# Three MLP down projections as seven block products a quarter (Strassen), with weight sums made on the chip

## The chip, the cores and the metric

One core of one Trainium2 chip runs the whole kernel in one launch. Times are device microseconds. The kernel before has a median of 2088.71 us over three runs (2087.34 to 2089.89). All sizes are float32; "fp32r" is the form in which TensorE takes a float32 operand in a single pass.

## The reference

Two layers of a first block and one layer of a second one work on x of 512 tokens by 1024 channels. Each layer ends in an MLP with 4096 hidden channels, and only the three MLPs are changed:

```python
# layers 0 and 1
h = rms_norm(x, norm_pre_mlp[i])
y = jnp.square(jax.nn.relu(h @ w_up[i])) @ w_down[i]
x = x + rms_norm(y, norm_post_mlp[i])
# layer 2 (the second block), then a last norm
hm = rms_norm_2(x, g_mlp[l])
x = x + jnp.square(jax.nn.relu(hm @ w_up[l])) @ w_down[l]
```

## The kernel before

A product of float32 accuracy is made from three passes (`mm3`): every operand is split into hi (its rounding, written by ScalarE) and lo (the exact rest, written by VectorE, `split` at L241 and L242), and hi·hi, hi·lo and lo·hi are added up in a bank of PSUM. A pass is a matmul of 128 x 128 by 128 x 512.

`mlp` takes the 4096 hidden channels in four quarters f of 1024. A quarter has an up phase of eight blocks of 128 channels (`project`; 8 x 24 = 192 matmuls), each followed by ScalarE's relu (L514), VectorE's square (L515) and a split into the `big` tiles, which hold the down product's stationary side. Then comes the down phase: four token tiles by two halves of 512 output columns, each over eight K-blocks in three passes, 8 x 24 = 192 matmuls into the banks named `acc`. In quarters 0 to 2 `out_gemm` runs one column half after the other; in quarter 3 `last_down` runs both halves of a token tile in turn, so that tile 0 is finished first. Weights come in chunks of 512 KB through three landing tiles ws and are split into WB = 4 pairs of tiles wh, wl. The queue of SyncE (SP) issues all loads.

In layers 0 and 1 the sums over quarters are kept in four tiles y (ScalarE's copy at f = 0, VectorE's `y += acc`, L536, after that). In quarter 3 each finished half is squared and summed (L319), multiplied by the gain (L542), and with both halves done `add_normed` takes GpSimd's power (L326) and adds y / rms to x (L469). `after` then runs the next mixer's norm of that token tile (L343), its transposes on TensorE (L267) and their split into h. `issue_late` sets where in TensorE's order a tile's transposes stand: those of tile t-1 behind the last product of tile t. In layer 2 the sums go straight into x (L527). Engines work their instructions in the order given, so a waiting instruction holds back everything behind it on its engine.

Of the kernel before, what the change touches and what calls it, by code (L numbers as in the profile page):

```python
# [20 lines left out]
NT = T // P  # L21
# [8 lines left out]
# ---------------------------------------------------------------- host layout  # L30
def ws(w):
    """[K, N] -> [N/128][128 of K][K/128 * 128 of N]: a block of columns as the stationary side."""
    k, n = w.shape
    return np.ascontiguousarray(
        w.reshape(k // P, P, n // P, P).transpose(2, 1, 0, 3)
    ).reshape(n // P, P, -1)


def xs(w, kt, n):
    """[K, N] -> [N/n][K/(128 kt)][128][kt * n]: a block of columns as the moving side."""  # L40
    k, nn = w.shape
    return np.ascontiguousarray(
        w.reshape(k // (kt * P), kt, P, nn // n, n).transpose(3, 0, 2, 1, 4)
    ).reshape(nn // n, k // (kt * P), P, kt * n)

# [30 lines left out]
def arrange(a):  # L76
# [22 lines left out]
    for i in range(2):  # L99
# [4 lines left out]
        o[f"wd{i}"] = xs(f["w_down"][i], 2, 512)  # L104
# [16 lines left out]
    o["wd2"] = xs(f["w_down_2"][0], 2, 512)  # L121
# [48 lines left out]
# ---------------------------------------------------------------- device  # L170
class Net:
# [21 lines left out]
    def load_x(self, src, gain=True, tiles=range(NT)):  # L193
        """x, and room for the gain of the next mixer's norm"""
# [13 lines left out]
    # -- small helpers  # L208
# [30 lines left out]
    def split(self, hi, lo, src, engine=None):  # L239
        """src = hi + lo: hi is src rounded to what one pass carries, lo the exact rest."""  # L240
# [19 lines left out]
    def mm(self, out, lhs, rhs, start, stop, more=False):  # L260
        """more: the bank's sums are added to again once they have been read"""
# [29 lines left out]
    def sooner(self, n):  # L291
        """the instructions within go before the n before them where both can"""
# [7 lines left out]
    def mm3(self, out, lhs, rhs, start, stop):  # L300
        """lhs, rhs: (hi, lo); out += lhs^T rhs to float32's accuracy."""
# [5 lines left out]
    # -- norms; np is the pool of their scratch  # L307
# [13 lines left out]
    def rstd(self, np_, ss):  # L321
        """ss: [128, 2], the halves' sums of squares / 1024 -> 1 / sqrt(mean + eps)"""
# [9 lines left out]
    def norming(self, np_, src, g, hi, lo, t, bank="tp", keep=True, junk=None):  # L332
        """src: the two halves of 128 rows; their normalised transpose goes to columns t of hi, lo."""
# [19 lines left out]
    def issue_late(self, t, last):  # L353
        """the transposes of token tile t go behind `last` in TensorE's order"""
# [14 lines left out]
    def prenorm(self, np_, gname, tiles, bank="tp", kept=False):  # L369
        """the normalised rows of x, transposed and split, tile by tile through the function it returns"""  # L370
# [8 lines left out]
    # -- matrix products  # L379
# [73 lines left out]
    def big_chunks(self, tp):  # L453
        """room for chunks of weights, two in a pair of big tiles"""
# [8 lines left out]
    # -- the end of a layer  # L463
    def add_normed(self, np_, t, yg, ss):
        """x += yg / rms, yg the products with the gain"""
        r = self.rstd(np_, ss)
        for j in range(2):
            x = self.xhalves(t)[j]
            self.nc.vector.scalar_tensor_tensor(out=x, in0=yg[:, j * 512:(j + 1) * 512], scalar=r, in1=x,  # L469
                                                op0=ALU.mult, op1=ALU.add)  # L470

    def mix_out(self, tp, wname, mixed, gname, corder, after, lead=3, store=True):
        """x += [norm of] mixed^T W_out"""
# [4 lines left out]
        for nh in range(2):  # L478
            def done(t, p):
# [3 lines left out]
                else:  # L483
                    if nh == 0:
                        y[t] = tp.tile([P, D], F32, name="y", tag="y", bufs=4)
# [16 lines left out]

    def mlp(self, tp, i, h, post, after):
# [3 lines left out]
        y, ss = {}, {}  # L507
        for f in range(4):
            u = [[tp.tile([P, 4, T], F32R, name="big", tag="big", bufs=8) for _ in range(2)] for _ in range(2)]

            def relu2(b, p):
                b -= f * 8
                r = tp.tile([P, T], F32, name="relu", tag="relu", bufs=2)
                nc.scalar.activation(r, p, AF.Relu)  # L514
                nc.vector.scalar_tensor_tensor(out=r, in0=p, scalar=0.0, in1=r, op0=ALU.max, op1=ALU.mult)  # L515
                self.split(u[b // 4][0][:, b % 4, :], u[b // 4][1][:, b % 4, :], r)
            self.project(f"wu{i}", range(f * 8, f * 8 + 8), h, relu2, 0 if f else 5)

            def lhs(k, t):
                c = slice(t * P, (t + 1) * P)  # L520
                return u[k // 4][0][:, k % 4, c], u[k // 4][1][:, k % 4, c]
            dones = []
            for nh in range(2):
                def done(t, p, f=f, nh=nh):
                    c = slice(nh * 512, (nh + 1) * 512)
                    if g is None:
# [1033 lines left out]
```

## Time and profile before

| | |
|---|---|
| runs shown | 2087.34, 2088.71, 2089.89 us |
| profiled execution: span | 2085.1 us |
| TensorE (PE) busy | 2050.3 us, 98% |
| VectorE (DVE) busy | 1184.1 us, 57% |
| ScalarE (ACT) busy | 949.4 us, 46% |
| GpSimd (POOL) busy | 111.8 us, 5% |
| bytes moved by DMA | 200.07 MB, mean 96 GB/s |

The span is that of one execution under the profiler; the runs shown are whole executions, and the median is 3.6 us above that span. "PE" rows are matmuls, "PEld" the loads of their stationary side, which overlap them. A matmul's own duration is its latency: the next one starts before it ends. In a timeline row with a count the second number is the time from the first start to the last end. DRAM traffic is far from filling the queues (one hardware queue carries 198.29 MB and is busy for 29.7% of the span).

### The profile page before, as it was taken

The numbers are of one execution on the slowest core, as the hardware profiler recorded it, in microseconds if no ns is written. First come the engines' busy times: TensorE is split into PE (matmuls) and PEld (weight loads), VectorE is DVE, ScalarE is ACT, GpSimd is POOL, SyncE is SP. The second block draws the span as 40 slices with busy tenths as digits, with TensorE's granted clock in tenths as the row PEclk, the third lists the DMA queues.
The fourth block names the chain that finished last, engine by engine and source line by source line (L and its number), as shares of the span: only waits on it lengthen the run. The fifth ranks groups of instructions, "written<-read, shape, count | busy, mean of one in ns | idle before, by whom it ended". The sixth has DMA issues, their size and how long they took to land.

```text
span 2085.1 us, 27806 instructions
## 1 busy us (share of the span) xinstructions
PE 2050.3 (98%) x10748; PEld 1727.7 (83%) x10748; DVE 1184.1 (57%) x2313; ACT 949.4 (46%) x1923; POOL 111.8 (5%) x190
## 2 busy tenths in 40 slices
PE   7999999999999999999999999999999999999998
PEld 6788887888888898878888888888788889888887
DVE  6969885524335656786434435688665555344343
ACT  5656664433324456784433324445654434233232
POOL 1211010000000001120000000000000000000000
PEclk9999999999999999999999999999999999999999
DMA  5222113332323321104233324231245232323331
GB/s 202 83 80 71 41 51 134 109 100 85 109 81 128 117 82 55 38 31 162 91 100 93 101 88 134 102 91 61 73 161 161 81 121 64 98 91 101 101 93 69
DMA packets 59605, 200.07 MB, mean 96 GB/s; under 512 B 7632, under 2 KB 8912, under 8 KB 59472
## 3 DMA queue, kind: packets, MB, share of 16 engines
q1 hardware_dynamic: 59472, 198.29, 29.7%
q8 instruction: 84, 1.38, 0.3%
q14 instruction: 49, 0.40, 0.1%
HBM read 191.45 MB, written 6.82 MB: 95 GB/s over the span
## 4 chain that ended last, share of the span: by engine, by line
PE 89%; DVE 6%; ACT 3%; issue 1%; POOL 1%; DMA 0%; SPq 0%; DVEq 0%; POOLq 0%; ACTq 0%
PE ps L263 45%; PE acc L263 34%; PE z L263 2%; PE s L263 1%; PE scan L263 1%; PE o L263 1%; PE tp L267 1%; DVE wl L242 1%; PE inv L263 1%; PE fa L263 1%; PE late L263 1%; DVE in L847 1%; PE acc L267 0%; DVE row L931 0%; POOL v L326 0%
## 5 line engine op out<-in xcount | busy, mean ns | idle before, releaser
L242 DVE TENSOR_TENSOR wl<-ws,wh 128x512 fp32r<-128x512 f32 (+1 forms) x525 | 396.3, 772 | 472.5 <-ACT wh L241 468.8
L241 ACT ACTIVATE wh<-ws 128x512 fp32r<-128x512 f32 (+1 forms) x527 | 353.4, 690 | 629.9 <-PE ps L263 333.9
L263 PE MATMUL ps<-big,wh 128*128 128x512 f32 (+1 forms) x1776 | 486.5, 361 | 0.3 <-DVE big L242 0.3
L263 PE MATMUL acc<-wh,big 128*128 128x512 f32 x1344 | 417.5, 389 | 0.0
L263 PEld LDWEIGHTS ps<-big,wh 128*128 128x128 f32 x1776 | 317.8, 189 | 51.4 <-DVE big L242 0.5
L263 PE MATMUL ps<-big,wl 128*128 128x512 f32 (+1 forms) x888 | 319.8, 361 | 0.0
L263 PE MATMUL ps<-h,wh 128*128 128x512 f32 (+1 forms) x1040 | 307.8, 379 | 1.5 <-ACT beta L801 0.9
L263 PEld LDWEIGHTS acc<-wh,big 128*128 128x128 f32 x1344 | 252.4, 188 | 52.1
L263 PE MATMUL acc<-wl,big 128*128 128x512 f32 x672 | 261.5, 389 | 0.0
L263 PEld LDWEIGHTS ps<-h,wh 128*128 128x128 f32 x1040 | 181.3, 191 | 31.9 <-issue 3.7
L263 PE MATMUL ps<-h,wl 128*128 128x512 f32 (+1 forms) x520 | 191.7, 369 | 0.0
L263 PEld LDWEIGHTS ps<-big,wl 128*128 128x128 f32 x888 | 167.6, 189 | 25.3
L263 PEld LDWEIGHTS acc<-wl,big 128*128 128x128 f32 x672 | 126.2, 188 | 26.3
L326 POOL TENSOR_TENSOR v<-v,mhalf 128x1 f32<-128x1 f32 x52 | 31.6, 608 | 1587.6 <-DVE v L325 1587.6
L263 PEld LDWEIGHTS ps<-h,wl 128*128 128x128 f32 x520 | 98.9, 190 | 16.2 <-issue 0.5
L263 PE MATMUL acc<-wh,h 128*128 128x512 f32 x320 | 105.5, 399 | 0.7 <-ACT a L1183 0.7
L536 DVE TENSOR_TENSOR y<-acc,y 128x512 f32<-128x512 f32 x48 | 33.1, 689 | 81.3 <-PE acc L263 81.1
L241 ACT ACTIVATE big<-relu 128x512 fp32r<-128x512 f32 x96 | 60.7, 633 | 34.6 <-DVE relu L515 34.6
L242 DVE TENSOR_TENSOR big<-relu,big 128x512 fp32r<-128x512 f32 x96 | 66.5, 693 | 11.2 <-ACT big L241 2.1
L263 PEld LDWEIGHTS acc<-wh,h 128*128 128x128 f32 x320 | 59.5, 188 | 13.2 <-ACT a L1183 1.3
L263 PE MATMUL acc<-big,h 128*128 128x512 f32 x288 | 67.7, 392 | 0.0
L263 PE MATMUL acc<-big 128*128 128x512 f32 x288 | 67.2, 389 | 0.0
(350 smaller groups left out, 2971.5 us busy)
## 6 DMA issues: line engine op xcount, KB each, us to landing
ws<-wu_dram SPq DMA_DIRECT2D x96, 512.0 KB, 4.0
ws<-wd_dram SPq DMA_DIRECT2D x96, 512.0 KB, 3.5
ws<-wia_dram SPq DMA_DIRECT2D x27, 512.0 KB, 3.6
ws<-wo_dram SPq DMA_DIRECT2D x24, 512.0 KB, 3.6
ws<-wi_dram SPq DMA_DIRECT2D x20, 512.0 KB, 3.6
ws<-wib_dram SPq DMA_DIRECT2D x14, 512.0 KB, 3.6
kept<-x SPq DMA_DIRECT2D x8, 512.0 KB, 2.6
ws<-wck_dram SPq DMA_DIRECT2D x8, 512.0 KB, 3.9
```

The source lines that it names most:

```text
L241: self.nc.scalar.activation(hi, src, AF.Copy)
L242: (engine or self.nc.vector).tensor_tensor(out=lo, in0=src, in1=hi.bitcast(F32), op=ALU.subtract)
L263: return self.nc.tensor.matmul(out, lhs, rhs, start=start, stop=stop or more, skip_group_check=more)
L267: return self.nc.tensor.transpose(out, src, self.ident)
L326: nc.gpsimd.tensor_tensor(out=v, in0=v, in1=self.mhalf, op=ALU.pow)
L536: nc.vector.tensor_tensor(out=y[t][:, c], in0=p, in1=y[t][:, c], op=ALU.add)
L847: nc.vector.scalar_tensor_tensor(out=o[:, s:], in0=p[:, :T - s], scalar=w[:, 3 - s:4 - s], in1=o[:, s:], op0=ALU.mult, op1=ALU.add)
```

## The change

Each quarter's down product is taken as a 2 x 2 block product: the operand (512 tokens by 1024 channels) in blocks a11, a12, a21, a22 of 256 tokens by 512 channels, the weights in blocks b11 to b22 of 512 channels by 512 columns. Seven products of such blocks, P0 to P6 (Winograd's form of Strassen's scheme), take the place of eight: each has two token tiles, four K-blocks and three passes, 2 x 4 x 3 = 24 matmuls of 512 columns, 168 a quarter. A table sets which weight class, which operand, which pair of banks (x, y, z) and which first target and sign each has; a bank that is used by several products keeps on adding and is read after each. The weights lie in DRAM as plain blocks; of the seven classes three are loaded (b11, b21, b22) and four (t1 to t4) are made by VectorE in place, by adding another plain load. Of the operand side four sums are made from each pair of up blocks (`combine`). A quarter loads 14 pieces of 512 KB in place of 8.

In layers 0 and 1 the old x is written to DRAM at the start of the MLP ("mid"), its four tiles take the sums y, and in quarter 3 it is fetched back into the tile named relu, two token tiles at a time; `add_normed` reads it there. Lines after are 9 to 100 higher: L242 is L251, L263 is L272, L267 is L276, L343 is L352, L469 is L478, L536 is L644, L542 is L650.

```diff
+    SCHEME = (("b11", "a11", "x", (0, 0, 1)), ("b21", "a12", "y", (0, 0, 1)), ("t1", "s1", "z", (1, 1, -1)),
+              ("b22", "S4", "z", (0, 1, -1)), ("t2", "S2", "x", (0, 1, -1)), ("t3", "S3", "x", (1, 1, -1)),
+              ("t4", "a22", "x", (1, 0, 1)))
...
+    def combine(self, r, ops, m):
...
+        split(0, 2)
+        sub(s1, a22, a21)
+        nsub(S2, s1, a11)
+        nsub(S4, S2, a12)
+        split(1, 2)
+        sub(S3, a11, a21)
+        split(2, 2)
+        split(3, 1)
...
+    def wclass(self, tp, wq, name, held):
...
+            if name in ("b11", "b21", "b22"):
+                s = tp.tile([P, D], F32, name="w" + tile_, tag="y", bufs=YB)
+                self.nc.sync.dma_start(s, wq[half, src])
+                held[tile_, half] = s
+            else:
+                s = held[tile_, half]
+                b = self.wp.tile([P, D], F32, name="ws", tag="ws", bufs=3)
+                self.nc.sync.dma_start(b, wq[half, src])
+                self.nc.vector.tensor_tensor(out=s, in0=s, in1=b, op=ALU.add)
...
+            self.split(h, l, s)
...
+    def quarter(self, tp, wq, ops, read):
...
+        ahead = [self.wclass(tp, wq, self.SCHEME[0][0], held)]
+        for n, (name, operand, bank, what) in enumerate(self.SCHEME):
+            if n + 1 < len(self.SCHEME):
+                ahead.append(self.wclass(tp, wq, self.SCHEME[n + 1][0], held))
+            w = ahead.pop(0)
...
+                    for x, y in ((0, 0), (0, 1), (1, 0)):
+                        last = self.mm(acc, lhs[x], w[half][y][:, c], first and m + x + y == 0, m == 3 and x == 1, True)
+                if half:
+                    read(p, acc, *what, n, last)
...
+            for t in range(NT):
+                nc.sync.dma_start(kept[t], self.x[t])
...
+                if f == 0 and n == [x[3][:2] for x in self.SCHEME].index((th, ch)):
+                    nc.scalar.activation(y[t][:, c], acc, AF.Copy, scale=float(sign))
+                else:
+                    nc.vector.tensor_tensor(out=y[t][:, c], in0=y[t][:, c], in1=acc, op=op)
...
+                if th != ch:
+                    self.add_normed(tp, t, y[t], ss[t], old[t])
+                    if t == 1:
+                        fetch(2)
+                    after(t)
...
+                if f == 3 and n >= 5:
+                    self.issue_late(n - 5, last) if p else None
```

VectorE, a quarter's down phase (f = 1 or 2) before: `wl` are low parts of weights for this phase and, later, the next up phase, `y<-acc,y` the eight reads of the banks.

```order
L536 TENSOR_TENSOR y<-acc,y 128x512 x3
L242 TENSOR_TENSOR wl<-ws,wh 128x512 x4
L536 TENSOR_TENSOR y<-acc,y 128x512
L242 TENSOR_TENSOR wl<-ws,wh 128x512 x4
L536 TENSOR_TENSOR y<-acc,y 128x512 x3
L242 TENSOR_TENSOR wl<-ws,wh 128x512 x4
```

VectorE, the same phase after: `wa`, `wc` are the two weight tiles in which the classes are made, `x_3398` to `x_3401` the four tiles with the sums.

```order
L644 TENSOR_TENSOR x_3400<-x_3400,acc 128x512
L564 TENSOR_TENSOR wa<-wa,ws 128x1024
L251 TENSOR_TENSOR wl<-wa,wh 128x1024
L644 TENSOR_TENSOR x_3401<-x_3401,acc 128x512
L251 TENSOR_TENSOR wl<-wa,wh 128x1024
L644 TENSOR_TENSOR x_3398<-x_3398,acc 128x512
L564 TENSOR_TENSOR wc<-wc,ws 128x1024 x2
L644 TENSOR_TENSOR x_3399<-x_3399,acc 128x512
L251 TENSOR_TENSOR wl<-wc,wh 128x1024 x2
L644 TENSOR_TENSOR x_3398<-x_3398,acc 128x512
```

Sums and low parts of 1024 columns now stand between the reads, and there are 14 reads where there were eight.

VectorE, the last quarter of layer 0 before: a tile's two reads, its gain, its norm and its h (`h<-tp`) follow each other, with nothing of the weights between.

```order
L536 TENSOR_TENSOR y<-acc,y 128x512
L242 TENSOR_TENSOR h<-tp,h 128x4x128
L542 TENSOR_TENSOR y<-y,g 128x512
L242 TENSOR_TENSOR h<-tp,h 128x4x128
L325 SCALAR_TENSOR_TENSOR v<-ss 128x1
L469 SCALAR_TENSOR_TENSOR x_3399<-y,v,x_3399 128x512 x2
```

VectorE, the last quarter of layer 0 after, from the norm of tile 0 to the read of P5's first bank (`x_3400<-x_3400,acc`), whose bank P6 adds to next.

```order
L564 TENSOR_TENSOR wa<-wa,ws 128x1024
L352 SCALAR_TENSOR_TENSOR wide<-x_3398,v,gk 128x512 x2
L478 SCALAR_TENSOR_TENSOR x_3399<-x_3399,v,relu 128x512 x2
L251 TENSOR_TENSOR h<-tp,h 128x4x128
L251 TENSOR_TENSOR wl<-wa,wh 128x1024
L251 TENSOR_TENSOR h<-tp,h 128x4x128
L334 SCALAR_TENSOR_TENSOR v<-ss 128x1
L644 TENSOR_TENSOR x_3400<-x_3400,acc 128x512
```

The norm of tile 0, the update of tile 1, tile 0's h and the low part of P6's weights now stand ahead of that read.

TensorE, the end of layer 0 before: the 24 matmuls of tile 3's second half (shown as one row where the names allow), then tile 2's transposes and the next mixer.

```order
L263 MATMUL acc<-wl,big 128x512
L263 MATMUL acc<-wh,big 128x512
L263 MATMUL acc<-big 128x512 x24
L267 MATMUL tp<-ident,wide 128x128 x8
L263 MATMUL ps<-h,wh 128x256 x2
```

TensorE, the same end after: first the end of P5 with tile 0's transposes and the start of P6.

```order
L272 MATMUL acc<-wl,big 128x512
L272 MATMUL acc<-wh,big 128x512
L276 MATMUL tp<-ident,wide 128x128 x8
L272 MATMUL acc<-wh,big 128x512
L272 MATMUL acc<-wl,big 128x512
```

Tile 0's transposes stand between P5 and P6 and tile 1's behind P6; those of tiles 2 and 3 fall into the next mixer.

## Rows read from the trace of the kernel before

**Rows 1.** The page's first part: busy us (share of the span) x instructions.

```profile
PE 2050.3 (98%) x10748; PEld 1727.7 (83%) x10748; DVE 1184.1 (57%) x2313; ACT 949.4 (46%) x1923; POOL 111.8 (5%) x190
```

**Rows 2.** Stretches of layer 0: us, busy (x count) by engine, PEclk, DMA share, GB/s.

```profile
core 0: us, PE busy (x) PEld busy (x) DVE busy (x) ACT busy (x) POOL busy (x), PEclk, DMA share, GB/s
453.00:496.50 43.50, 43.50 (x194) 36.03 (x193) 20.31 (x32) 17.67 (x32) 0.00 (x0) 1.00 0.39 120
496.50:540.00 43.50, 43.50 (x194) 36.03 (x193) 15.33 (x24) 10.19 (x18) 0.00 (x0) 1.00 0.24 74
670.70:716.90 46.20, 46.20 (x218) 38.46 (x216) 31.34 (x50) 20.73 (x45) 3.30 (x6) 1.00 0.34 115
```

**Rows 3.** TensorE's timeline around one product: start us, us, engine, line, operation, tiles.

```profile
676.17 5.60 PE L263 MATMUL acc<-big 128*128 128x512 f32 x24
681.61 0.39 PE L263 MATMUL acc<-wh,big 128*128 128x512 f32 x1
```

**Rows 4.** Groups by form: count | busy us, mean ns | idle before, releaser.

```profile
L242 DVE TENSOR_TENSOR wl<-ws,wh 128x512 fp32r<-128x512 f32 x448 | 299.4, 687 | 430.9 <-ACT wh L241 428.9
L242 DVE TENSOR_TENSOR wl<-ws,wh 128x1024 fp32r<-128x1024 f32 x77 | 96.9, 1263 | 41.6 <-ACT wh L241 39.8 <-PE ps L263 1.6
L241 ACT ACTIVATE wh<-ws 128x1024 fp32r<-128x1024 f32 x79 | 83.5, 1057 | 61.1 <-PE ps L263 43.8 <-issue 7.0 <-PE s L263 3.2
L536 DVE TENSOR_TENSOR y<-acc,y 128x512 f32<-128x512 f32 x48 | 33.1, 689 | 81.3 <-PE acc L263 81.1
L242 DVE TENSOR_TENSOR ll<-t,lh 128x256 fp32r<-128x256 f32 x12 | 5.2, 436 | 2.2 <-ACT lh L241 2.1
```

**Rows 5.** VectorE's timeline where it works without a gap, end of layer 0.

```profile
674.38 1.89 DVE L242 TENSOR_TENSOR big<-ws,big 128x512 fp32r<-128x512 f32 x3
676.37 0.69 DVE L536 TENSOR_TENSOR y<-acc,y 128x512 f32<-128x512 f32 x1
...
709.58 2.36 DVE L242 TENSOR_TENSOR wl<-ws,wh 128x1024 fp32r<-128x1024 f32 x2
...
715.80 1.22 DVE L242 TENSOR_TENSOR wl<-ws,wh 128x1024 fp32r<-128x1024 f32 x1
```

**Rows 6.** DMA issues: xcount, KB each, us from issue to landing.

```profile
ws<-wd_dram SPq DMA_DIRECT2D x96, 512.0 KB, 3.5
kept<-x SPq DMA_DIRECT2D x8, 512.0 KB, 2.6
```

**Rows 7.** The norm of token tile 0 at the end of layer 0, timeline.

```profile
682.60 0.63 ACT L319 ACTIVATE junk<-y 128x512 bf16<-128x512 f32 x1 [3.68 <-DVE y L536]
683.96 0.15 DVE L325 SCALAR_TENSOR_TENSOR v<-ss 128x1 f32<-128x1 f32 x1
684.26 0.55 POOL L326 TENSOR_TENSOR v<-v,mhalf 128x1 f32<-128x1 f32 x1 [314.54 <-DVE v L325]
684.84 1.41 DVE L469 SCALAR_TENSOR_TENSOR x<-y,v,x 128x512 f32<-128x512 f32 x2 [0.73 <-POOL v L326]
```

**Rows 8.** TensorE's timeline from the last up product to the next mixer's start.

```profile
670.50 0.39 PE L263 MATMUL ps<-big,wl 128*128 128x512 f32 x1
716.09 1.03 PE L267 MATMUL tp<-ident,wide 128*128 128x128 f32 x8
716.88 0.48 PE L263 MATMUL ps<-h,wh 128*128 128x256 f32 x2
725.60 1.04 PE L267 MATMUL tp<-ident,wide 128*128 128x128 f32 x8
```

**Rows 9.** TensorE's timeline in the first 25 us, with its two waits.

```profile
8.83 1.54 PE L267 MATMUL tp<-ident,wide 128*128 128x128 f32 x6 [8.83 <-DVE wide L343]
15.68 0.41 PE L263 MATMUL ps<-h,wl 128*128 128x256 f32 x1
18.07 0.28 PE L263 MATMUL ps<-h,wl 128*128 128x256 f32 x1
24.16 1.34 PE L267 MATMUL late<-ident,x 128*128 128x128 f32 x8 [1.49 <-issue]
```

More of the change, by code (lines that the diff above doesn't have):

```diff
@@ L169 @@
 LAG_E=1
+YB=5
 class Net:
@@ new lines, in operand_tiles @@
+    def operand_tiles(self, tp):
+        tiles = [self.hp.tile([P, 4, T], F32R, name="h", tag="h", bufs=4) for _ in range(4)]
+        tiles += [tp.tile([P, 4, T], F32R, name="big", tag="big", bufs=8) for _ in range(4)]
+        views = [t.rearrange("p a n -> p (a n)").rearrange("p (s m c) -> p s m c", s=2, m=4) for t in tiles]
+        return views[::2], views[1::2]
+    def combine(self, r, ops, m):
+        nc = self.nc
+        a11, a12, S4, s1, S2, S3, a22, a21 = (r[:, j, :] for j in range(8))
+        sub = lambda out, a, b: nc.vector.tensor_tensor(out=out, in0=a, in1=b, op=ALU.subtract)
+        nsub = lambda out, a, b: nc.vector.scalar_tensor_tensor(out=out, in0=a, scalar=-1.0, in1=b, op0=ALU.mult,
+                                                                op1=ALU.subtract)
+        split = lambda g, n: self.split(ops[0][g][:, :n, m, :], ops[1][g][:, :n, m, :], r[:, 2 * g:2 * g + n, :])
+        split(0, 2)
[6 more added lines that the diff above has]
+        split(3, 1)
@@ new lines, in wclass @@
+    def wclass(self, tp, wq, name, held):
+        tile_, src = self.CLASS[name]
+        out = []
+        for half in range(2):
+            if name in ("b11", "b21", "b22"):
[7 more added lines that the diff above has]
+                self.nc.vector.tensor_tensor(out=s, in0=s, in1=b, op=ALU.add)
+            h = self.wp.tile([P, D], F32R, name="wh", tag="wh", bufs=WB)
+            l = self.wp.tile([P, D], F32R, name="wl", tag="wl", bufs=WB)
+            self.split(h, l, s)
+            out.append((h, l))
+        return out
@@ new lines, in quarter @@
+    def quarter(self, tp, wq, ops, read):
+        held, banks = {}, {}
+        ahead = [self.wclass(tp, wq, self.SCHEME[0][0], held)]
[3 more added lines that the diff above has]
+            w = ahead.pop(0)
+            g, s = divmod(self.OPERANDS.index(operand), 2)
+            places = [(half, p) for half in range(2) for p in range(2)] if n == 0 else [
+                (half, p) for p in range(2) for half in range(2)]
+            for half, p in places:
+                if (bank, p) not in banks:
+                    banks[bank, p] = self.bank("acc")
+                acc = banks[bank, p]
+                first = n == [x[2] for x in self.SCHEME].index(bank)
+                for j in range(2):
+                    m, c = half * 2 + j, slice(j * 512, (j + 1) * 512)
+                    t = slice(p * P, (p + 1) * P)
+                    lhs = tuple(o[g][:, s, m, t] for o in ops)
+                    last = None
+                    for x, y in ((0, 0), (0, 1), (1, 0)):
+                        last = self.mm(acc, lhs[x], w[half][y][:, c], first and m + x + y == 0, m == 3 and x == 1, True)
+                if half:
+                    read(p, acc, *what, n, last)
@@ L506, in mlp, with fetch @@
         g = self.gain(tp, post) if post else None
-        y, ss = {}, {}
+        ss, old, y = {}, {}, self.x
+        if g:
+            kept = self.dram.tile([NT, P, D], F32, name=f"mid{i}")
+            for t in range(NT):
+                nc.sync.dma_start(kept[t], self.x[t])
+        def fetch(t):
+            r = tp.tile([P, 8, T // 2], F32, name="relu", tag="relu", bufs=1).rearrange("p a n -> p (a n)")
+            for j in range(2):
+                old[t + j] = r[:, j * D:(j + 1) * D]
+                nc.sync.dma_start(old[t + j], kept[t + j])
@@ L508, in mlp @@
+        final = {(th, ch): n for n, (_, _, _, (th, ch, _)) in enumerate(self.SCHEME)}
         for f in range(4):
-            u = [[tp.tile([P, 4, T], F32R, name="big", tag="big", bufs=8) for _ in range(2)] for _ in range(2)]
+            ops = self.operand_tiles(tp)
+            pair = {}
             def relu2(b, p):
                 b -= f * 8
-                r = tp.tile([P, T], F32, name="relu", tag="relu", bufs=2)
+                if b % 2 == 0:
+                    pair[0] = tp.tile([P, 8, T // 2], F32, name="relu", tag="relu", bufs=1)
+                r = pair[0][:, 0::7, :] if b % 2 == 0 else pair[0][:, 1::5, :]
+                p = p.rearrange("p (a n) -> p a n", a=2)
@@ L514, in relu2 @@
                 nc.scalar.activation(r, p, AF.Relu)
                 nc.vector.scalar_tensor_tensor(out=r, in0=p, scalar=0.0, in1=r, op0=ALU.max, op1=ALU.mult)
-                self.split(u[b // 4][0][:, b % 4, :], u[b // 4][1][:, b % 4, :], r)
+                if b % 2:
+                    self.combine(pair[0], ops, b // 2)
             self.project(f"wu{i}", range(f * 8, f * 8 + 8), h, relu2, 0 if f else 5)
-            def lhs(k, t):
-                c = slice(t * P, (t + 1) * P)
-                return u[k // 4][0][:, k % 4, c], u[k // 4][1][:, k % 4, c]
@@ L568, in mem_load, with reads @@
+            if f == 3:
+                self.late = {}
+                if g:
+                    fetch(0)
+            def reads(p, acc, th, ch, sign, n, last, f=f):
+                read(p, acc, th, ch, sign, n, last)
+                if f == 3 and n >= 5:
+                    self.issue_late(n - 5, last) if p else None
+            self.quarter(tp, self.I[f"wd{i}"][f], ops, reads)
     def mem_load(self, pool, np_, src, gname):
```

75 lines of the change are left out of this document (29 added, 46 removed).

## The prediction

> **What bounds the kernel now.** I read the page's first part first: TensorE is busy for 98% of the span, VectorE for 57%, ScalarE for 46% [rows 1]. So time goes where matmuls go, as long as nothing new makes TensorE wait. Next the stretches of one quarter [rows 2]: in an up phase (43.5 us) and a down phase (43.5 us) TensorE is busy without a break; VectorE works 20.3 and 15.3 us of them, ScalarE 17.7 and 10.2, and the DMA share is 0.39 and 0.24. VectorE's waits are for ScalarE's hi parts and for the banks (428.9 and 81.1 us) [rows 4]: it is the one that waits. Last the end of a layer (the third stretch) [rows 2, 8]: VectorE is busy 31.3 of 46.2 us there, with norms, and is the nearest to a bound.
>
> **TensorE's saving.** 24 matmuls take 681.61 - 676.17 = 5.44 us from their first start to the next product's [rows 3], 0.2267 us each. A quarter's down phase goes from 192 to 168 of them, 43.5 to 38.1 us. Twelve quarters: 288 x 0.2267 = 65.3 us. Up phases and mixers keep theirs. A time of 65 us less needs the rest to stay hidden.
>
> **Cost of VectorE's new work, quarters 0 to 2 (nine of them).** I use the pace of back-to-back instructions: 512 columns (1.89 - 0.69)/2 = 0.60 us, 1024 columns 2.36 - 1.22 = 1.14, taken as 1.13 (0.13 less than a single one) [rows 5]; single ones take 0.69 and 1.26 [rows 4]; 128 x 256 about 0.34 (0.436 less the same 0.09). The sum `s = s + b` isn't in the trace. Its nearest row is the low part of the same size, also two operands from SBUF to SBUF: 1.13. As bounds, 1.13 and two instructions of half the size unpaced, 2 x 0.69 = 1.38; I take 1.13, the same shape. Between the end of the up phase and the last product VectorE has 11 low halves (12.4), 6 sums (6.8), 14 reads (8.4), the last pair's square, combination and lows (3.8), and 6 lows for the next up phase (3.6): 35.0 us of work in 38.1. Upper bound of the sums: + 1.5, still 36.5. In the up phase the other 3 low halves, 2 sums and the combinations bring it to about 27 of 43.5 us.
>
> That leaves 3.1 us spare, so order decides. I laid the queues of the four engines and SP by hand beside each other, instruction by instruction in the changed order, with these durations, ScalarE's 1.06 for a hi half [rows 4], 3.5 us for a load [rows 6] and 0.04 us from an end to the waiting start. One wait comes out: in P0 the last block of a11, whose hi waits behind ScalarE's hi for t1, is ready at 4.6 us where TensorE wants it at 4.1. The phase takes 38.6 us: gain 43.5 - 38.6 = 4.9 a quarter, nine times: 44.5 us.
>
> ScalarE gets 14 hi halves of 1.06 = 14.8 us a phase and stays half idle. Loads: 14 of 512 KB in place of 8, 3.5 us each, through three landing tiles; in the walk t3's second comes at 15.4 and is wanted at 21.5, t4's second at 25.3, wanted at 27.2. Hidden, with 2 us to spare at the tightest; if each t4 were 3.5 us late instead, 1.6 us a quarter would go. Parking x is four writes of 2.6 us [rows 6], on a queue whose next loads are already ahead by the landing tiles: 0, at most 2 x 4 x 2.6 = 21 us if nothing hid them. I take 0, as the eight writes of the same kind before made TensorE wait nowhere. The fetches are issued over 10 us before they are read.
>
> **The ends of layers 0 and 1.** Here a moved wait costs. Before, the banks are read in the order of the tiles, and TensorE has a whole product between. After, VectorE's order puts the norm of tile 0, the update of tile 1, tile 0's h and P6's low part ahead of the read of P5's bank x, which P6 adds to. Along the queue (0 = last up product): P4's first read 25.5; sum for t4, low part, gain and power; the update of tile 0 at 29.9 to 31.4, its norm only at 34.5 to 35.9 (a tile's chain square, v, power, update is 682.60 to 686.25, 3.65 us, when nothing is in between [rows 7], and is run twice). TensorE ends P5 at 33.1, waits 2 us, does tile 0's transposes (0.79 us, 716.88 less 716.09 [rows 8]) to 36.6, waits until the read at 39.7 to 40.3 is over, and runs P6 from 40.4 instead of 33.1. P6 ends at 45.9, tile 1's transposes at 47.0, its h is split by 50.3. Before, the next mixer's first matmul started 716.88 - 670.73 (the start after 670.50) = 46.15 us after the last up product [rows 8]; now 50.3, 4.1 us later. But before, tile 2's transposes were already in that stretch; now they cost the mixer 1.1 us more, and tile 3's norm, late by the same queue, another 1.8 us at its transposes. So each end loses 7.1 us instead of gaining 5.44: 14.2 us lost.
>
> In layer 2 the norms of tiles 0 and 1 stand in front of the read likewise, but no update goes before them (the sums lie in x already): P6 starts at 34.8 instead of 33.1, and what follows the last product is as before. Gain about 3.3.
>
> Sum: 44.5 + 3.3 - 14.2 = 33.6 us, so the span goes from 2085.1 to 2051.5 and the time, with 3.6 us around it, to 2055 us: 1.6% faster.
>
> **A rule that speaks against it.** The pace used above shows only where VectorE's instructions follow each other [rows 5]; in this kernel a single one takes 0.69 and 1.26 us [rows 4]. The Trainium skill ("VectorE: DVE Perf Modes", section "The TRN2 errata — SBUF-src ops pay a fixed extra latency per instruction") says that a fixed latency is exposed between instructions, and that a float32 addition of N elements takes (N + 151)/0.96 ns; an estimate by it is 1.22, 0.69 and 0.42 us for 1024, 512 and 256 columns, and 17 x 1.22 + 24 x 0.69 + 4 x 0.42 = 39.0 us of VectorE's work in 38.1. In rows 5 the gap between starts is smaller than the duration, so the trace contradicts full exposure there, with waits long over; no run here shows it for waits that end late. That is a rival below.
>
> **Rivals.**
> *1. VectorE pays its single duration each time.* The same list with 0.69, 1.26 and 0.44: 17 x 1.26 + 24 x 0.69 + 4 x 0.44 = 39.7 us against 38.1, so VectorE is the bound, by 1.6 us, and the ends stretch too. By the walk at 10% longer instructions a quarter gains 4.1, each end loses 11.3 and layer 2 gains 1.3: 37 + 1.3 - 22.6 = 15.5, 2073 us. For it: in the changed order nearly every VectorE instruction stands behind another engine's work (a read behind TensorE, a low part behind ScalarE, a sum behind a load). Against it: the runs of two and three in rows 5 are low parts, each behind ScalarE's hi, and keep the pace. Range 2064 to 2084.
> *2. The order does not hold TensorE at the ends,* because the norm's chain is shorter than I have it or the reads come sooner: the ends gain 0 to 5 us each instead of losing 7, and 2055 becomes 2024 to 2042. Against it: the read stands behind the norm in VectorE's order, and that is fixed.
> *3. TensorE slows down after the waits at the ends.* After its 8.83 us wait at the start, matmuls of 256 columns ran 0.21 us apart until about 17.6 us and 0.12 after; after the 1.49 us wait at 24.16 nothing slowed [rows 9]. The new waits (2.0, 3.8 and 3.3 us) lie between these two. If a wait at each end brought as long a slow stretch as that first one (17.6 - 8.8 = 8.8 us at about half pace), it would lose 4.4 us an end: 2055 becomes 2055 to 2064, the clock's column being 1.00 so far [rows 2]. The Trainium skill ("TensorE: Matmul & The Clock Gate", section "Part 1: The HAM clock gate") says that an idle TensorE falls from 2.4 to 1.2 GHz, as that start of the kernel agrees with; a wait of 3.8 us is not shown here.
> *4. Slower than before.* The one mechanism is VectorE's queue as the bound of all twelve down phases: from about 9% longer instructions than the pace, every 1% costs a quarter 0.35 us (35.0 x 1%) and each end 0.4. At 15% the walk gives no gain: 9 x 2.6, less 2 x 13.4, + 0.3 = -3 us, 2092. At 20%: 9 x 1.1 - 2 x 15.5 - 0.7 = -22, 2110 us. It would take VectorE being slowed by the seven extra megabytes of loads per quarter, or by one more wait per read. Against it: in the up phase, at a DMA share of 0.39, VectorE's 32 instructions took 20.31 us = 0.63 each, in the down phase at 0.24, 24 took 15.33 = 0.64 [rows 2]; no slowing with DMA.
>
> That the change does not remove the matmuls can be left out: 288 are gone from the program.
>
> **Chances.** Forecast, 2044 to 2064: 0.47, the third rival within it or just beside: 0.12; first rival 0.19; second 0.12; slower 0.08; the rest, within 0.2% of before (about what a measurement of this kernel tells from no change), 0.02. So faster 0.90, same 0.02, slower 0.08. The range leaves out the slow case (0.1 above) and half of the second rival (0.06 to 0.08 below): 2036 to 2082. The likeliest is 2055.
>
> **What would show it.** Matmuls into acc: 2016 of 512 columns with big and h as operands, 0.2267 apart, in place of 2304. A steady down phase of 38 to 39 us with VectorE busy near 92%, in place of 43.5 at 35%; a first wait in it of about 0.5 us. Sums of about 1.2 us each. At the ends of layers 0 and 1, TensorE waits of 2, 4 and 3 us, before tile 0's transposes for the norm, before P6 for the read of P5's bank, and before the mixer for h. A phase of 40 us or more with waits at many products shows the first rival; P6 starting within 1 us of P5's end shows the second; matmuls of 512 columns 0.4 us apart after the waits show the third. The forecast is wrong if sums or reads take more than 1.3 and 0.75 us, or if TensorE waits for loads of the t classes.

## The result, and the profile after

The changed kernel has a median of 2057.33 us (2056.13 to 2057.89, four runs) against 2089.29 for the kernel before: a ratio of 0.9847 with an interval of 0.9833 to 0.9861, 1.5% faster. The forecast was 2055 us. The profiled execution's span is 2055.3 us in place of 2085.1. The page's first part of the kernel after, which answers to [rows 1]:

```profile
PE 1997.5 (97%) x10460; PEld 1675.4 (82%) x10460; DVE 1514.5 (74%) x2745; ACT 1054.5 (51%) x1995; POOL 115.1 (6%) x190
```

TensorE has lost 288 matmuls and VectorE has gained 330 us of work. Stretches of the kernel after: the third up phase and the third down phase of layer 0, and the 50 us behind the last up product of layer 0. They answer to [rows 2].

```profile
core 0: us, PE busy (x) PEld busy (x) DVE busy (x) ACT busy (x) POOL busy (x), PEclk, DMA share, GB/s
531.33:574.85 43.52, 43.52 (x193) 36.04 (x192) 29.39 (x50) 18.77 (x33) 0.00 (x0) 1.00 0.37 115
574.85:613.24 38.39, 38.39 (x170) 31.38 (x168) 34.42 (x43) 17.48 (x22) 0.00 (x0) 1.00 0.52 173
...
656.76:706.76 50.00, 43.09 (x185) 34.30 (x183) 46.34 (x64) 26.63 (x46) 3.08 (x4) 0.93 0.45 147
```

A steady down phase takes 38.39 us in place of 43.52, with TensorE busy throughout and VectorE busy 34.42 us (90%). At the end of the layer VectorE is busy 46.34 of 50 us and TensorE stands idle for 7 of them. The groups by form and the pace show the new work (line, engine, operation, tiles, count | busy us, mean ns | idle before, releaser):

```profile
L251 DVE TENSOR_TENSOR wl<-wa,wh 128x1024 fp32r<-128x1024 f32 x96 | 116.6, 1220 | 32.1 <-ACT wh L250 31.9
...
L564 DVE TENSOR_TENSOR wa<-wa,ws 128x1024 f32<-128x1024 f32 x72 | 87.0, 1217 | 0.1
...
L644 DVE TENSOR_TENSOR x<-x,acc 128x512 f32<-128x512 f32 x96 | 64.9, 681 | 1.4 <-PE acc L272 1.4
```

and from VectorE's timeline of the third down phase of layer 0, two sums, a read and two low parts:

```profile
600.74 2.35 DVE L564 TENSOR_TENSOR wa<-wa,ws 128x1024 f32<-128x1024 f32 x2
603.01 0.68 DVE L644 TENSOR_TENSOR x<-x,acc 128x512 f32<-128x512 f32 x1
603.61 2.35 DVE L251 TENSOR_TENSOR wl<-wa,wh 128x1024 fp32r<-128x1024 f32 x2
```

Starts are 2.27 us apart for two sums, 1.13 each, and 0.60 for a read: the paces of [rows 5]. TensorE's waits at the end of layer 0, from its timeline (the last column is the wait and what ended it):

```profile
692.22 1.32 PE L276 MATMUL tp<-ident,wide 128*128 128x128 f32 x8 [2.29 <-DVE wide L352]
697.30 0.77 PE L272 MATMUL acc<-wh,big 128*128 128x512 f32 x1 [3.76 <-DVE x L644]
...
704.87 1.03 PE L276 MATMUL tp<-ident,wide 128*128 128x128 f32 x8
706.86 0.50 PE L272 MATMUL ps<-h,wh 128*128 128x256 f32 x2 [0.95 <-ACT h L250]
```

Counted from 656.76, where the last up product is over, P6 starts at 40.5 us (forecast 40.4) and the mixer at 50.1 (50.3). Layer 1's end shows the same waits.

Where the time went, by the starts of the first down products of each quarter in the two traces:

| term | forecast | measured, us |
|---|---|---|
| nine steady down phases | -44.5 (38.6 each) | 38.38 each: -46.2 |
| layer 0's end, to layer 1's first down product | +7.1 | 365.57 - 358.87 = +6.7 |
| layer 1's end, to layer 2's | +7.1 | 489.09 - 482.57 = +6.5 |
| layer 2's end, from its last up product | -3.3 | 52.49 - 50.65 = +1.8 |
| up to the first down product | 0 | 411.07 - 409.61 = +1.5 |
| sum | -33.6 | -29.7 |

The last term need not be an effect of the change: in the runs below, park4 apart, that point lies between 408.8 and 412.5 us, for most kernels with the same instructions up to there. The first norm waits for its gain, which lands at another time in each execution: it starts at 8.02 us in the trace before and at 9.12 in the one after, 1.1 of the 1.5 us.

### The profile page after: what moved, and what is told of

Read it like the earlier page. It is cut to its first block, busy times and chain, and to the rows that moved or that the text cites. A ratio compares the mean times of both kernels' runs of the same rounds, so it can differ in the third digit from the quotient of the medians.

```text
span 2055.3 us, 27912 instructions
## 1 busy us (share of the span) xinstructions
PE 1997.5 (97%) x10460; PEld 1675.4 (82%) x10460; DVE 1514.5 (74%) x2745; ACT 1054.5 (51%) x1995; POOL 115.1 (6%) x190
## 4 chain that ended last, share of the span: by engine, by line
PE 85%; DVE 8%; ACT 4%; POOL 1%; issue 1%; DMA 0%; SPq 0%; DVEq 0%; POOLq 0%; ACTq 0%
PE ps L272 45%; PE acc L272 29%; PE z L272 2%; DVE wl L251 2%; PE scan L272 1%; PE s L272 1%; PE o L272 1%; PE inv L272 1%; POOL v L335 1%; PE tp L276 1%; PE fa L272 1%; DVE wide L352 1%; DVE x L478 1%; DVE in L947 1%; ACT wh L250 1%
## 5 line engine op out<-in xcount | busy, mean ns | idle before, releaser
L272 PE MATMUL ps<-big,wh 128*128 128x512 f32 (+1 forms) x1776 | 486.6, 361 | 0.3 <-DVE big L251 0.3
L251 DVE TENSOR_TENSOR wl<-ws,wh 128x512 fp32r<-128x512 f32 (+1 forms) x357 | 284.2, 814 | 229.2 <-ACT wh L250 226.7
L250 ACT ACTIVATE wh<-ws 128x512 fp32r<-128x512 f32 (+1 forms) x359 | 250.1, 720 | 307.2 <-PE ps L272 201.2
L272 PEld LDWEIGHTS ps<-big,wh 128*128 128x128 f32 x1776 | 317.7, 189 | 51.4 <-DVE big L251 0.5
L272 PE MATMUL acc<-wh,h 128*128 128x512 f32 x1088 | 347.2, 395 | 0.7 <-ACT a L1283 0.7
L272 PE MATMUL ps<-big,wl 128*128 128x512 f32 (+1 forms) x888 | 319.8, 361 | 0.0
L272 PE MATMUL ps<-h,wh 128*128 128x512 f32 (+1 forms) x1040 | 308.3, 379 | 4.1 <-ACT h L250 1.9
L272 PEld LDWEIGHTS acc<-wh,h 128*128 128x128 f32 x1088 | 202.7, 188 | 48.9 <-ACT h L250 3.6
L272 PE MATMUL acc<-wl,h 128*128 128x512 f32 x544 | 212.7, 391 | 0.0
L272 PEld LDWEIGHTS ps<-h,wh 128*128 128x128 f32 x1040 | 181.4, 191 | 35.4 <-issue 3.7
L272 PE MATMUL acc<-wh,big 128*128 128x512 f32 x576 | 184.5, 398 | 9.8 <-DVE x L644 7.5
L272 PE MATMUL ps<-h,wl 128*128 128x512 f32 (+1 forms) x520 | 191.7, 369 | 0.0
L272 PEld LDWEIGHTS ps<-big,wl 128*128 128x128 f32 x888 | 167.6, 189 | 25.4
L251 DVE TENSOR_TENSOR wl<-wa,wh 128x1024 fp32r<-128x1024 f32 x96 | 116.6, 1220 | 32.1 <-ACT wh L250 31.9
L272 PEld LDWEIGHTS acc<-wh,big 128*128 128x128 f32 x576 | 110.8, 192 | 34.7 <-ACT wh L250 8.4
L272 PEld LDWEIGHTS acc<-wl,h 128*128 128x128 f32 x544 | 102.2, 188 | 20.4 <-issue 0.2
L272 PE MATMUL acc<-wl,big 128*128 128x512 f32 x288 | 114.2, 396 | 0.0
L272 PEld LDWEIGHTS ps<-h,wl 128*128 128x128 f32 x520 | 98.9, 190 | 16.2 <-issue 0.5
```

Of the source, the lines that this page charges most:

```text
L250: self.nc.scalar.activation(hi, src, AF.Copy)
L251: (engine or self.nc.vector).tensor_tensor(out=lo, in0=src, in1=hi.bitcast(F32), op=ALU.subtract)
L272: return self.nc.tensor.matmul(out, lhs, rhs, start=start, stop=stop or more, skip_group_check=more)
```

## The experiments

Theory A, that of the forecast: the ends of the layers lose because VectorE's order puts norms ahead of a bank's read and of P6's weights. Theory B: they lose through what surrounds the products. The steady phases were tried by adding known work.

**plain_last.** Eight plain products in each last quarter.

```diff
+            plain = f == 3
...
-            self.quarter(tp, self.I[f"wd{i}"][f], ops, reads)
+            if not plain:
+                self.quarter(tp, self.I[f"wd{i}"][f], ops, reads)
+                continue
...
+            for t in range(NT):
+                for nh in range(2):
...
+                        last = self.mm3(acc, x, (w[0][:, m:m + 512], w[1][:, m:m + 512]), k == 0, k == 7)
```

> The last quarter of each MLP takes its down product in eight plain block products as before (192 matmuls, tile by tile), the other three quarters stay at seven; x stays parked in DRAM. Theory A (the last quarter loses because VectorE's order puts norms ahead of bank reads that TensorE waits for): the ends go back to those of the kernel before, which were 6.7, 6.5 and 1.8 us shorter than those after: 2057.3 - 15 = 2042 us, no TensorE wait over 1 us in these quarters, the clock column at 1.00 there. Theory B (the ends lose through what surrounds the products: the fetch of x, the slow stretch of TensorE, the two-tile finish of the mixer): less than half of it, 2050 us or more.

2045.45 us (2042.63 to 2047.64), ratio 0.979 (0.9776 to 0.9805): 12 us faster than the change. The mixer starts 46.1 us after the last up product in both layers, and layer 2's end takes 50.75 us: by these starts the ends are back at their length before, 15 us in all, though x is still parked and fetched. Part of it was taken back elsewhere: in its profile TensorE ran at the lower of its two levels, 1.2 GHz, for 20.5 us in layer 1's mixer, which took 7.9 us more than before:

```profile
895.00:905.00 10.00, 10.00 (x33) 7.98 (x33) 6.62 (x13) 6.48 (x15) 1.94 (x6) 0.50 0.00 0
```

That the last quarter's seven products are a loss is shown, and that parking x is not what costs it; not yet by which of their parts.

**reads_first.** Reads and weights ahead of the norms, in the last quarter.

```diff
+                with self.sooner(300 if f == 3 else 0):
+                    nc.vector.tensor_tensor(out=y[t][:, c], in0=y[t][:, c], in1=acc, op=op)
...
+                with self.sooner(ahead_by):
+                    ahead.append(self.wclass(tp, wq, self.SCHEME[n + 1][0], held))
```

> All seven products stay in the last quarter; in VectorE's order there the reads of banks and the making of weights go ahead of the norms (300 instructions earlier where they can), which also moves the transposes of tile 0 to the end of P6. Theory A: P6 starts within 1 us of P5's end in place of 7.3 us later, each end of layers 0 and 1 gains 3 to 5 us, as the norms are then late instead; layer 2's end gains 4 to 6 (no wait of 1.9 us, no slow stretch of 1.7, the read of P6's second bank ahead of tile 2's norm, 1.8): 2041 to 2048 us. Theory B: P6 starts on time but the mixer starts no sooner: layers 0 and 1 gain under 1 us each, 2051 us or more.

2053.99 us, ratio 0.984 (0.982 to 0.986). P6 now starts without a wait, but the 5.5 us come back before the transposes of tile 1, in TensorE's timeline of this kernel (its last up product ends at 656.64):

```profile
686.17 0.47 PE L272 MATMUL acc<-wh,big 128*128 128x512 f32 x1 [0.53 <-DVE x L647]
697.39 0.66 PE L276 MATMUL tp<-ident,wide 128*128 128x128 f32 x4 [0.29 <-DVE wide L352]
704.26 1.94 PE L276 MATMUL tp<-ident,wide 128*128 128x128 f32 x8 [5.54 <-DVE wide L352]
```

The mixer starts at 49.4 us, and each end gains 0.5 and 0.3 us; layer 2's, which has no mixer behind it, gains 2.9. VectorE is busy 47.31 of the 50 us. P6 runs at the higher level here; a stretch of 6.8 us at 1.2 GHz begins in the wait of 5.54 us and falls on the mixer's start instead. So Theory A falls for layers 0 and 1: the order decides where TensorE waits, and hardly how long. Theory C takes its place, to be tried below: the amount of VectorE's work up to the mixer's start sets the ends.

**dose6 and dose2.** Known work added to VectorE in the steady phases: low parts computed a second time.

```diff
+            if self.more and name in ('b22', 't2', 't3'):
+                self.nc.vector.tensor_tensor(out=l, in0=s, in1=h.bitcast(F32), op=ALU.subtract)
```

> In the first three quarters of each MLP six low parts of weights a quarter (classes b22, t2, t3) are computed twice on VectorE, the second time with the same result: 6 x 1.13 = 6.8 us more of VectorE's work in each such down phase, all of it ahead of P6's weights. If VectorE's spare time is what the page after shows (38.39 - 34.42 = 4.0 us, some 2.7 of it before P6): each of the nine phases takes 3 to 5 us longer, 41.5 to 43.5 in place of 38.4, together 27 to 45 us, 2085 to 2102. Rival, VectorE has time to spare all the way: under 1 us a phase. Rival, VectorE already sets the phase: 6.8 us a phase, 61 us together, 2118.

> As the run with six, but only class t3's two low parts are computed twice: 2.26 us more of VectorE's work in each of the nine down phases. If the spare time is 2.7 us before P6: 0 to 0.4 us a phase, phases of 38.4 to 38.8, 2057 to 2061 us. Rival, VectorE already sets the phase: 2.3 us a phase, 40.6 each, 2078.

dose6 took 2105.68 us and dose2 (class t3 alone) 2070.57, one run each. By the nine steady quarters 6.8 us more work cost 4.5 us a phase on average, and 2.26 us cost 0.8. But the nine are of two kinds. In the first quarters of layers 0 and 1 ScalarE makes eight of the fourteen reads as copies, VectorE has as many less, and the doses cost 1.5 and 0.0 us. In the other seven dose2 costs 1.0 us each, so that 1.3 of 2.26 are hidden; dose6 costs 4.0 to 6.5, the 4.0 in the one of them without a stretch at 1.2 GHz, so that 2.8 of 6.8 are hidden there. Of the 4.0 us in which VectorE stands still in such a phase, 1.3 to 2.8 can be used, by where the work stands. With dose2 the one wait is not for weights: P5 waits for the read of P4's bank, which stands behind the added work (with dose6 it waits 2.8 us for its weights).

```profile
603.50 0.47 PE L272 MATMUL acc<-wh,big 128*128 128x512 f32 x1 [0.72 <-DVE x L646]
```

The rest of dose2's time is not the dose: its mixer of layer 1 ran at 1.2 GHz for 20.5 us like that of plain_last, and took 8.4 us more.

**nosum_last.** The last quarter without its eight sums.

```diff
-                self.nc.vector.tensor_tensor(out=s, in0=s, in1=b, op=ALU.add)
+                if self.last:
+                    s = b
+                else:
+                    self.nc.vector.tensor_tensor(out=s, in0=s, in1=b, op=ALU.add)
```

> In the last quarter of each MLP the eight sums of weight blocks are left out (the four t classes there are the plain loads, so the output is not the reference's); all seven products, splits, reads and norms stay. Theory C, formed after the run with the reads first (the ends of layers 0 and 1 are bound by how much VectorE has to do until the mixer can start, 46.4 of 50 us, not by its order): 6 x 1.13 = 6.8 us less work moves the mixer's start from 50.1 us after the last up product to 43 to 46 in each, layer 2 gains 2 to 4 us: 2040 to 2046 us. Theory A in its first form (the order of reads and norms and the latency of the norm's chain): the mixer starts less than 2 us sooner, 2050 us or more.

2046.54 us, one run. The mixer starts at 42.8 us, 7.3 sooner, a little more than Theory C says. But it waits again for VectorE, which still has the mixer's own weights to split behind the norms:

```profile
697.42 0.50 PE L272 MATMUL ps<-h,wh 128*128 128x256 f32 x2 [0.25 <-ACT h L250]
698.55 0.51 PE L272 MATMUL ps<-h,wh 128*128 128x256 f32 x2 [0.50 <-DVE h L251]
702.20 0.58 PE L272 MATMUL ps<-h,wl 128*128 128x256 f32 x1 [3.04 <-DVE wl L251]
```

The ends gain 2.2, 3.6 and 2.6 us in all.

**light_last.** Without the sums and without the t classes' low parts.

```diff
+            if self.last and name[0] == "t":
+                self.nc.scalar.activation(h, s, AF.Copy)
+                out.append((h, h))
+                continue
```

> In the last quarter of each MLP both the eight sums and the eight low parts of the t classes are left out (their hi parts stand in for the low ones; the output is not the reference's): 16 x 1.13 = 18 us less of VectorE's work, TensorE's products, ScalarE's work and the norms unchanged. Theory C in full (only the amount of VectorE's work in the last quarter sets the ends): the mixer starts at 41 to 43 us after the last up product and waits no more than 1 us for VectorE after that; layers 0 and 1 end 8 to 12 us sooner each than after the change, 2030 to 2038 us. Theory E (part of the loss is that tiles 2 and 3 are finished only with the last product, so that their norms and the mixer's own weights meet on VectorE behind it): the mixer starts at 41 to 43 us but loses 2 to 4 us again in its first 15 us to VectorE, as without sums; 2040 to 2047 us.

2039.74 us, one run. The mixer starts at 41.5 us; the ends gain 6.4, 6.3 and 3.8 us. That is between the two theories' times, but the mixer then waits 3.3 us for VectorE, as Theory E has it, where Theory C allowed 1. With 18 us of VectorE's work gone, its busy time in the 50 us is 35.3, near plain_last's 34.0, and the ends of layers 0 and 1 are just as long as with eight products (359.2 and 482.8 us against 358.9 and 482.6 before), though TensorE has 5.4 us less to do. What is left are TensorE's waits, 3.9 us in all, for norms and h of the later tiles and for a low part of the mixer's weights:

```profile
696.19 1.29 PE L276 MATMUL tp<-ident,wide 128*128 128x128 f32 x8 [0.62 <-DVE wide L352]
699.16 0.39 PE L272 MATMUL ps<-h,wh 128*128 128x256 f32 x1 [1.03 <-DVE h L251]
704.01 0.39 PE L272 MATMUL ps<-h,wl 128*128 128x256 f32 x1 [1.36 <-DVE wl L251]
712.45 0.63 PE L276 MATMUL tp<-ident,wide 128*128 128x128 f32 x4 [0.87 <-DVE wide L352]
```

So an end of layers 0 and 1 misses its 5.4 us and loses 6.6 more, 12 us; 6.4 of them come with VectorE's work on the weights of the t classes, and the other 5.7 remain without it. The 6.4 hold what TensorE's lower level costs behind the waits (P6 ran partly at 1.2 GHz in the kernel after; light_last has no such stretch at these ends). That the 5.7 lie in tiles 2 and 3 being finished only by P6 fits the waits, but no run finished them sooner with seven products.

**gp_last and gp_all.** Sums on GpSimd, in the last quarters or everywhere.

```diff
-                self.nc.vector.tensor_tensor(out=s, in0=s, in1=b, op=ALU.add)
+                (self.nc.gpsimd if self.on_gp else self.nc.vector).tensor_tensor(out=s, in0=s, in1=b, op=ALU.add)
```

> The eight sums of the last quarter are made by GpSimd instead of VectorE; the other quarters stay. An estimate from GpSimd's products of 128x512 (1.58 us each in the profile after): 3.2 us a sum, 19 us of the 38 in that phase. Theory C: VectorE has 6.8 us less to do and the mixer starts 3 to 6 us sooner at the ends of layers 0 and 1, layer 2 gains 2 to 4 us: 2041 to 2048. Rival: GpSimd's power of the norm queues behind its sums, or GpSimd slows VectorE, and the gain is gone: 2053 us or more.

> All sums of weight blocks, in every quarter, are made by GpSimd. With 3.2 us a sum (estimate as in the run with the last quarter alone) they are ready 3 us or more before each product wants them: steady phases stay at 38.4 us, as TensorE sets them, and the ends gain as in that run: 2041 to 2048 us. Rival: a sum on GpSimd takes longer beside VectorE's work, or slows VectorE; then steady phases grow by 1 to 5 us each: 2060 to 2095.

gp_last took 2070.44 us (one run), its ends 3.9, 5.2 and 5.0 us longer than with the sums on VectorE; gp_all took 2115.83 with a ratio of 1.0144 (1.0111 to 1.0177), slower than the kernel before the change. A sum takes GpSimd 2.5 us, sooner than estimated, but VectorE's low part beside it does not go on. The two engines' timelines in gp_all, VectorE and then GpSimd:

```profile
596.56 0.67 DVE L644 TENSOR_TENSOR x<-x,acc 128x512 f32<-128x512 f32 x1
597.16 3.04 DVE L251 TENSOR_TENSOR wl<-wc,wh 128x1024 fp32r<-128x1024 f32 x1
...
604.26 3.02 DVE L251 TENSOR_TENSOR wl<-wa,wh 128x1024 fp32r<-128x1024 f32 x1
```

```profile
596.72 2.39 POOL L564 TENSOR_TENSOR wa<-wa,ws 128x1024 f32<-128x1024 f32 x1 [3.90 <-DVE wl L251]
...
603.81 2.38 POOL L564 TENSOR_TENSOR wc<-wc,ws 128x1024 f32<-128x1024 f32 x1 [1.16 <-DVE wl L251]
```

The low part that starts at 597.16 ends 1.09 us after GpSimd's sum (599.11), nearly its usual length of 1.22: it waited the sum out. The read of a bank that starts at 596.56, one operand in PSUM, runs beside the same sum and keeps its 0.67 us. Most steady phases take about 43.3 us.

**dma_sums and dma_sums_first.** The second load adds to the tile itself; the latter kernel has the order of reads_first as well.

```diff
-                b = self.wp.tile([P, D], F32, name="ws", tag="ws", bufs=3)
-                self.nc.sync.dma_start(b, wq[half, src])
-                self.nc.vector.tensor_tensor(out=s, in0=s, in1=b, op=ALU.add)
+                self.nc.gpsimd.dma_start(s, wq[half, src], accum_op=ALU.add)
```

> All weight sums are made by the loads themselves: GpSimd starts each second load as one that adds to the tile in SBUF, so VectorE makes no sums in any quarter and GpSimd computes none. Theory C (VectorE's amount of work sets the ends): steady phases stay at 38.4 us, and the ends gain what they gained without sums in the last quarter (2.2, 3.6 and 2.6 us): 2047 to 2050 us. Theory D, formed after the runs with GpSimd's sums (anything in which GpSimd touches SBUF beside VectorE slows VectorE, its low parts took 2.6 us in place of 1.2): low parts longer than 1.3 us and phases of 40 us or more: 2070 or more. If only the adding loads are late (a load that adds may be slower than the 3.5 us of a plain one), low parts stay at 1.2 us and TensorE waits before P4, P5 or P6.

> Sums made by adding loads in every quarter, and the reads and weights ahead of the norms in the last quarter. If the ends still lose to VectorE's work behind the last product, the order gives no more than the 0.3 to 0.5 us it gave alone at layers 0 and 1, and 1 to 3 us at layer 2: 2048 to 2052 us. If order and amount help each other, each end of layers 0 and 1 gains 2 us or more over the run with adding loads alone: 2047 or less.

2052.78 us (0.9828, 0.9811 to 0.9844) and 2049.45 (0.9815, 0.9798 to 0.9831). The adding loads (from GpSimd's queue, POOLq) and VectorE's low parts in dma_sums:

```profile
wa<-wd_dram POOLq DMA_DIRECT2D x72, 512.0 KB, 5.5
wc<-wd_dram POOLq DMA_DIRECT2D x24, 512.0 KB, 6.6
L251 DVE TENSOR_TENSOR wl<-wa,wh 128x1024 fp32r<-128x1024 f32 x96 | 117.2, 1222 | 77.7 <-ACT wh L250 77.5
```

They land in 5.5 to 6.6 us, against 4.1 to 4.5 for the plain loads beside them and 3.5 before the change, and TensorE's steady phases do not wait for them; low parts keep 1.22 us, phases 38.4 us. So Theory D is refuted. VectorE is busy 27.3 of 38 us there, and nothing is gained by it, as TensorE sets these phases. The ends gain 2.6, 1.1 and 0.8 us, in layer 1 and layer 2 less than Theory C's 3.6 and 2.6; why is open. With the reads first they gain 2.9, 3.7 and 3.1: the order adds 0.3 us in layer 0, but 2.6 in layer 1 and 2.3 in layer 2. The time lies in the range expected without help from the order, the ends agree with neither case in full.

**park4.** Four times the writes of x.

```diff
+            for more in range(4):
+                kept = self.dram.tile([NT, P, D], F32, name=f"mid{i}_{more}")
+                for t in range(NT):
+                    nc.sync.dma_start(kept[t], self.x[t])
```

> In layers 0 and 1 the old x is written to DRAM four times instead of once at the start of the MLP (12 more writes of 512 KB a layer; the last is the one fetched). If the writes are hidden, as the forecast had it: the first up phase of these layers and the time stay within 1 us, 2056 to 2059. Rival, the loads behind them on SyncE's queue come late: 12 x 2.6 = 31 us a layer at most, 2070 to 2119.

2068.95 us, one run, and neither as expected nor as the rival. From the first up product to the first down product layer 0 takes 50.8 us (363.71 to 414.52) in place of 48.9 (362.21 to 411.07), 1.9 more for 12 more writes; layer 1 takes 47.1 as it did. In its trace the mixer of layer 1 again ran at 1.2 GHz for 20.5 us, and layer 0's end took 8.5 us more. So four writes are hidden in both layers, sixteen in layer 1 alone.

**plain_two.** plain_last for layers 0 and 1, reads_first for layer 2 (`plain = f == 3 and g is not None`).

> Eight plain products in the last quarter of layers 0 and 1 as in the run with plain last quarters, seven products with the reads first in the last quarter of layer 2 as in the run with the reads first. By the phases of these two runs: ends of layers 0 and 1 as before the change, layer 2's end 49.6 us in place of 50.8: 1.2 us less than the run with plain last quarters, 2041 to 2046 us, the spread being that of stretches in which TensorE runs at half level in layer 1's mixer. If the ends do not add up like this: 2047 or more.

2045.19 us (2042.42 to 2047.88), 0.979 (0.9776 to 0.9805): layer 2's end takes 49.5 us, as added up, but the medians of this kernel and plain_last can't be told apart. They are the fastest kernels here that leave nothing out.

## Why the prediction was right, and where it was not

*TensorE's saving* and *VectorE's cover* were right: 5.13 us a steady phase by trace against 4.9 (the wait of 0.5 us expected in P0 did not come), sums at the pace of low parts. The first rival, single durations, is refuted by the same rows. Its list gave 39.7 us of work, the trace has 34.42 with 35.0 forecast. The prediction said that the order decides how much of the spare 3.1 us can be used; the doses found 1.3 us where the read of a shared bank comes due first. The up phase has 29.4 us of VectorE's work in place of 27.

*The ends of layers 0 and 1* were right in size and place, 6.7 and 6.5 us lost against 7.1, with waits of 2.3, 3.8 and 1.0 us against 2.0, 3.8 and 3.3. That the mixer's start agrees so well is in part luck: P6 took 7.6 us in place of 5.4, and the wait for h was 2.3 us shorter than forecast. The reason given was not right: "VectorE's order puts the norm of tile 0 ... ahead of the read" is what happens, but with the order turned round the mixer started only 0.7 us sooner. The amount of VectorE's work on weights is half of it (light_last). The second rival (reads sooner, no loss) rested on the same reason and falls with it.

*Layer 2's end* is the step that failed, by 5.1 us, a gain of 3.3 forecast and a loss of 1.8 measured: "what follows the last product is as before". P6 waited until 35.7 us in place of 34.8. It then ran partly at 1.2 GHz, 1.7 us. And the last read came late, behind tile 2's norm. The kernel after, first TensorE's two waits, then VectorE, then ScalarE's squares:

```profile
2033.67 0.50 PE L272 MATMUL acc<-wh,big 128*128 128x512 f32 x1 [0.43 <-DVE x L637]
2038.56 0.47 PE L272 MATMUL acc<-wh,big 128*128 128x512 f32 x1 [1.87 <-DVE x L637]
...
2046.33 1.41 DVE L1644 SCALAR_TENSOR_TENSOR wide<-x,v,g 128x512 f32<-128x512 f32 x2 [0.73 <-POOL v L335]
2047.66 0.68 DVE L637 TENSOR_TENSOR x<-x,acc 128x512 f32<-128x512 f32 x1
2049.94 0.16 DVE L334 SCALAR_TENSOR_TENSOR v<-ss 128x1 f32<-128x1 f32 x1 [1.60 <-ACT junk L328]
...
2048.43 0.63 ACT L328 ACTIVATE junk<-x 128x512 bf16<-128x512 f32 x1 [3.02 <-DVE x L637]
2049.19 0.63 ACT L328 ACTIVATE junk<-x 128x512 bf16<-128x512 f32 x1
```

The kernel before, where the last matmul ends at 2078.09:

```profile
2078.13 0.69 DVE L527 TENSOR_TENSOR x<-acc,x 128x512 f32<-128x512 f32 x1 [4.75 <-PE acc L263]
...
2078.91 0.63 ACT L319 ACTIVATE junk<-x 128x512 bf16<-128x512 f32 x1 [4.71 <-DVE x L527]
```

After the change TensorE's last matmul ends at 2045.87, the read starts 1.8 us later, and two halves' squares follow where it was one: 9.5 us from the last product to the end in place of 7.0. 0.9 + 1.7 + 2.5 = 5.1.

*The third rival* came true in part: after the waits TensorE ran at the lower level for part of P6 in all three layers. Stretches of layer 0's and layer 2's P6, columns as above:

```profile
697.00:704.00 7.00, 6.70 (x21) 5.40 (x22) 6.24 (x9) 1.74 (x5) 0.25 (x1) 0.67 0.66 224
2035.00:2042.00 7.00, 5.13 (x18) 3.85 (x17) 3.57 (x5) 0.00 (x0) 1.37 (x1) 0.83 0.20 75
```

In layers 0 and 1 P6 took 2.1 us longer by it, and tile 1's transposes follow P6 without a wait; how much sooner the mixer would start at the higher level no run shows. In layer 2 it cost the 1.7 us. The Trainium skill ("TensorE: Matmul & The Clock Gate", "Part 1: The HAM clock gate") has an idle TensorE fall to 1.2 GHz, and the trace agrees: the fall in layer 0 came after waits of 2.3 and 3.8 us with only eight transposes between. In layer 2 it came 1 us after P6 had begun, behind waits of 0.4 and 1.9 us.

*The fourth rival* (VectorE slowed by the loads) did not come: at a DMA share of 0.52 low parts take 1.22 us and the phase 38.39. The loads grew by six pieces, 3 MB a quarter, not by the seven megabytes that it names.

*Parking x* cost nothing, as forecast: layer 0's first up phase takes 48.86 us in both traces.

*The time* came closer than its terms. By the table the saving is 3.9 us short: steady phases gave 1.7 more and the ends of layers 0 and 1 gave 1.0 more, layer 2 gave 5.1 less and the start 1.5. The time is only 2.3 us off since the forecast added 3.6 us to its span, where the median after lies 2.0 above the profiled span. That part is luck.

## What to carry to other kernels

Count the work that a change adds to a second engine apart for each stage, not over the span: filling VectorE to 90% of a steady stage cost nothing there, and the same kind of work in the stage that also holds the norms cost 6.4 us, more than the 5.4 us of matmuls saved. If reordering moves a wait without shortening the stretch, suspect the engine's amount of work, and leave some of it out in a run: here that gave back half of the loss. The last round of a loop may be worth another algorithm than the rest: here plain products there are worth 12 us.

## What the runs showed of the hardware that was not expected

- VectorE's low part, two operands in SBUF, stood still while GpSimd added two tiles in SBUF: 3.04 us in place of 1.22; a read of PSUM beside it kept 0.67.
- In dma_sums a load of 512 KB that adds to a tile in SBUF lands in 5.5 to 6.6 us and leaves VectorE's 1.22 us as they are.
- In layer 1's mixer TensorE ran at 1.2 GHz for 14 to 20 us in the profiles of plain_last, plain_two, dose6, dose2 and park4, and in none of the others. It cost some 8 us each, 5.0 in plain_two. What brings it about is open; TensorE was busy all through the row shown.
